# Placing all activation slots of a two-layer encoder in one stretch of SBUF

## The chip, the cores and the metric

The kernel runs on one core of one Trainium2 chip. The metric is the device time of one execution in microseconds. Beside the timed runs there is one profiled execution, whose trace is read below.

## What is computed

A conformer-style encoder with two layers on 256 positions of width D = 2048, all in float32:

```python
for i in range(2):
    h = rmsnorm(x, mix_norm[i])
    if i == 0:   # GLU convolution module: D -> 2D, 31 taps per channel, layernorm, silu, D -> D
        u = h @ w_in + b_in;  u = a * sigmoid(gate);  u = causal_dwconv31(u)
        m = silu(layernorm(u)) @ w_out + b_out
    else:        # differential attention, 16 heads, T5 bias, chunked mask
        m = diff_attention(h, w_qkv, ...) @ w_o
    x = x + m
    h = rmsnorm(x, ffn_norm[i])
    u = causal_dwconv3(h @ w_up)            # D -> 2 * 5632
    x = x + (silu(gate) * val) @ w_down     # 5632 -> D
return rmsnorm(x, final_norm_g)
```

## The kernel before

Activations lie channels by positions: a tile of 128 channels x 256 positions. Every large product is made in split precision. A float32 weight tile `raw` (128 x 1024, 512 KB) comes by DMA on SP's queue; ScalarE rounds it to `hi` (L160) and VectorE, or GpSimd in the convolution, stores the rest as `lo` (L164). An activation is split the same way into one tile of 128 x 2 x 256, the rounded part and the rest side by side (`split_act`, L290 and L291). Such a tile fills one activation slot of 2048 bytes a partition.

`pair` makes 256 output channels in one group of matmuls. For each of the 128 input channels and each half j it issues a main matmul (`hi` against all 512 columns of the activation tile, L249) and a correction (`lo` against the first 256, L250); for the last input tile the order is turned round (L246, then L247). A weight tile serves four input tiles and is one step. A group over the 16 input tiles has 4 steps and 32 main/correction couples; in the FFN's down projection a group has 8 input tiles and 16 couples (4 and 8 in the first chunk). The convolution's input projection uses three matmuls of 256 columns instead (L240).

In order the stages are: input projection and convolution, layernorm, output projection (8 groups), first FFN, attention, its output projection (8 groups), second FFN. An FFN has 44 groups up and six chunks of 8 groups down, interleaved: one chunk's 8 groups up, then the previous chunk's 8 groups down. All steps stand in one list; the framework's scheduler turns it into one order per engine and sets the waits.

Slots come from two pools. `acta` has 25 slots and is opened early. When it has none left (during the first output projection), `act_tile` closes the convolution's pool `ph1` and opens `ph2` (tables and tiles of attention) and `actb`, 8 more slots, in the place that the convolution had. From then on a tile takes a slot of `acta` if one is free, otherwise one of `actb`; the trace names them act and actb. At most 33 slots are in use.

Of the kernel before, what the change touches and what calls it, by code (L numbers as in the profile page):

```python
# [8 lines left out]
F32 = mybir.dt.float32  # L9
# [5 lines left out]
P = 128  # L15
S = 256
# [3 lines left out]
FK = 3  # L20
# [5 lines left out]
class Cfg:  # L26


    def __init__(self, d, f, kc=4):
        self.D, self.F = d, f  # L30
        self.KT = d // P
        self.FT = f // P
        self.H = d // (2 * HD)
        self.KC = kc
        self.NW = kc * 256
        self.kcs = [(i, kc) for i in range(0, self.KT, kc)]
        full = self.KT // 2
        first = self.FT % full or full
        self.chunks = [(0, first)] + [(i, full) for i in range(first, self.FT, full)]
        self.VK = kc // 2  # L40
        self.NA, self.NB = self.KT + self.KT // 2 + 1, 8

        self.G = [3] * (self.KT - 3) + [5, 6, 0]

        self.ND = 16
# [16 lines left out]
class Builder:  # L62
    def __init__(self, ctx, tc, cfg, a):
        self.tc, self.nc, self.c, self.a = tc, tc.nc, cfg, a
        ec = ctx.enter_context
        self.ctx = ctx
        self.const = ec(tc.tile_pool(name="const", bufs=1))
        self.rawp = ec(tc.tile_pool(name="rawp", bufs=5))
        self.hip = ec(tc.tile_pool(name="hip", bufs=6))
        self.lop = ec(tc.tile_pool(name="lop", bufs=6))  # L70
        self.acta = ec(tc.tile_pool(name="acta", bufs=cfg.NA))
        self.sm = ec(tc.tile_pool(name="sm", bufs=2))
        self.pp = ec(tc.tile_pool(name="pp", bufs=2, space=bass.MemoryType.PSUM))
        self.px = ec(tc.tile_pool(name="px", bufs=1, space=bass.MemoryType.PSUM))
        self.dr = ec(tc.tile_pool(name="dr", bufs=1, space=bass.MemoryType.DRAM))
        self.ph1_stack = ExitStack()
        self.ph1 = self.ph1_stack.enter_context(tc.tile_pool(name="ph1", bufs=2))
        self.actb = None
        self.na, self.nb = cfg.NA, 0
        self.coloff, self.ncol = cfg.cols()  # L80
        self.steps, self.W, self.todo = [], [], {}
        self.s = self.n = self.np_ = self.ns = 0
        self.every = self.pool_first = None
# [4 lines left out]


    def b2(self, tag, dt=F32):  # L90
        return self.sm.tile([P, 2, S], dt, tag=tag, name=self.nm(tag), bufs={"E": 4, "Y": 4, "Z": 2, "A": 2}[tag])

    def b1(self, tag):
        return self.sm.tile([P, S], F32, tag=tag, name=self.nm(tag), bufs={"G": 4, "O": 3, "M": 3}[tag])
# [17 lines left out]


    def act_tile(self, dt=F32R):
        if self.na > 0:
            self.na -= 1
            return ("a", self.acta.tile([P, 2, S], dt, tag="act", name=self.nm("act")))
        if self.actb is None:
            self.ph1_stack.close()
            self.ph2 = self.ctx.enter_context(self.tc.tile_pool(name="ph2", bufs=1))  # L120
            self.actb = self.ctx.enter_context(self.tc.tile_pool(name="actb", bufs=self.c.NB))
            self.nb = self.c.NB
        assert self.nb > 0
        self.nb -= 1
        return ("b", self.actb.tile([P, 2, S], dt, tag="actb", name=self.nm("actb")))

    def free(self, tiles):
        for w, _ in tiles:
            if w == "a":
                self.na += 1  # L130
            else:
                self.nb += 1


    def load_w(self):
# [275 lines left out]
    def setup(self, n0):  # L411
        nc, c, a = self.nc, self.c, self.a
        KT = c.KT
        self.X = [self.const.tile([P, 2, S], F32, name=f"x{pr}") for pr in range(KT // 2)]
        o1, o2 = self.coloff["cw"][0], self.coloff["cb"][0]
        self.prm = self.const.tile([P, self.ncol - o2 + o1], F32, name="prm")
        self.cprm = self.ph1.tile([P, o2 - o1], F32, name="cprm", bufs=1)
        nc.scalar.dma_start(self.prm[:, :o1], a["prm"][:, :o1])
        self.ones = self.const.tile([P, P], F32, name="ones")
        nc.vector.memset(self.ones, 1.0)  # L420
        nc.scalar.activation(self.c2(), self.ones[:, 0:2], AF.Sigmoid)
        self.mhalf = self.const.tile([P, 2], F32, name="mhalf")
        nc.vector.memset(self.mhalf, -0.5)

        warm = self.psx("t", [P, P])
        for _ in range(7):
            nc.tensor.matmul(warm, self.ones, self.ones, start=True, stop=True)
        for pr in range(KT // 2):
            if self.np_ < 5:
                list(self.load_w())  # L430
            (nc.scalar if pr < 2 else nc.sync).dma_start(self.X[pr], a["x"][:, 2 * pr:2 * pr + 2, :])
        self.ident = self.const.tile([P, P], F32, name="ident")
        nc.sync.dma_start(self.ident, a["ident"])
        nc.sync.dma_start(self.cprm, a["prm"][:, o1:o2])
        self.cmask = self.const.tile([P, 32], F32, name="cmask")
        nc.sync.dma_start(self.cmask, a["cmask"])
        nc.sync.dma_start(self.prm[:, o1:], a["prm"][:, o2:])
        with self.tc.manual_schedule(engines={ET.DVE, ET.Activation, ET.Pool}):
            for m in range(KT):
                if m in (0, 2):  # L440

                    first = self.split_w() if m == 0 else first
                    next(first)
                elif m % 4 == 0 and m < 12:
                    self.ahead(self.ns)
                n0["xh"][m] = self.act_tile()
                self.split_act(n0["xh"][m][1], self.X[m // 2][:, m % 2, :], self.col("mixg", m))
                if m % 4 == 3 and m < 12:
                    self.ahead(self.ns)
                if m % 4 == 3 and m > 4:  # L450
                    for pr in (m // 2 - 3, m // 2 - 2):
                        self.x_square(n0, pr)
            for pr in (KT // 2 - 2, KT // 2 - 1):
                self.x_square(n0, pr)

        self.todo[7] = [lambda: self.norm_cols(n0)]
        self.todo[8] = [lambda: self.norm_rows(n0)]
        self.fpad = []
        for i in range(2):
            t = self.const.tile([P, 2, S + FK - 1], F32, name=f"fpad{i}")  # L460
            nc.vector.memset(t[:, :, 0:FK - 1], 0.0)
            self.fpad.append(t)
        self.cpad = []
        for i in range(4):
            t = self.ph1.tile([P, S + CK + 1], F32, name=f"cpad{i}", bufs=1)
            nc.vector.memset(t[:, 0:CK - 1], 0.0)
            nc.vector.memset(t[:, S + CK - 1:], 0.0)
            self.cpad.append(t)


    def conv_module(self, nin, nout):
        c, a = self.c, self.a
        nc = self.nc
# [196 lines left out]
        def layernorm():  # L670
# [24 lines left out]
            nc.vector.tensor_tensor(mr, mean, rc, ALU.mult)  # L695

            rp = [self.psx("s", [P, S]) for _ in range(2)]
            rs = self.b2("E")
            for x, v in enumerate((rc, mr)):
                self.rows(rp[x], v)  # L700
# [129 lines left out]
    def attn_setup(self):  # L830

        nc, c, a = self.nc, self.c, self.a
        H = c.H
        rb = self.ph2.tile([NB, H], F32, name="rb")
        self.tc.keep_in_program_order(nc.gpsimd.dma_start(rb, a["relb"]))
        oh = self.b2("Z").rearrange("p a s -> p (a s)")[:NB, :384]
        nc.gpsimd.dma_start(oh, a["oneh"])
        ps = self.psx("o", [P, 384])
        nc.tensor.matmul(ps[:H, :], rb, oh, start=True, stop=True)
        tb = self.b2("Z").rearrange("p a s -> p (a s)")[:H, :384]  # L840
        nc.vector.tensor_copy(tb, ps[:H, :])
        tab = self.dr.tile([H, 384], F32, name="tab")
        nc.gpsimd.dma_start(tab, tb)
# [320 lines left out]
```

## Time and profile before

| what | value |
|---|---|
| median of 3 runs | 2229.67 us (2228.4 to 2231.36) |
| profiled execution, its own time | 2228.45 us |
| its span from first to last instruction | 2226.7 us |
| mean granted clock of TensorE | 0.997 |
| TensorE (PE) matmuls busy | 2202.7 us, 99% of the span |
| weight loads (PEld) busy | 1935.3 us, 87% |
| VectorE (DVE) busy | 1629.1 us, 73% |
| ScalarE (ACT) busy | 1200.9 us, 54% |
| GpSimd (POOL) busy | 251.1 us, 11% |
| HBM traffic | 187 GB/s over the span |

Matmuls overlap, and their ends in the trace are modelled; how fast the stream runs is read from the starts. Outside the span lie 1.75 us of the profiled execution's time.

### The profile page before, as it was taken

To read this page: it belongs to the slowest core of one execution; us is meant where nothing else is said; L and a number is where in the kernel's file an instruction comes from. 1 tells how busy PE (TensorE), PEld (TensorE's weight loads), DVE (VectorE), ACT (ScalarE), POOL (GpSimd) and SP (SyncE) were. 2 spreads that over 40 slices of the span, in tenths; PEclk is the share of its full clock that TensorE was granted. 3 is DMA by queue.
4 is the path that set the end of the run, shared out by engine and by line. 5 is a ranking of instruction groups with operands and counts; after the bars stand their busy time and mean duration, and the time that the engine had idled before them with its cause. 6 is when DMAs were issued, how large, how long until landed. Compare 5 with 4: busy or idle time off the path is not lost.

```text
span 2226.7 us, 34566 instructions
## 1 busy us (share of the span) xinstructions
PE 2202.7 (99%) x13274; PEld 1935.3 (87%) x13274; DVE 1629.1 (73%) x2482; ACT 1200.9 (54%) x1799; POOL 251.1 (11%) x175
## 2 busy tenths in 40 slices
PE   9999899999999999999999999999999999999998
PEld 8899788888888888888888888888888888888887
DVE  5888777787767677677687778767777677776774
ACT  5333555555555455555565555555555455554554
POOL 2987510000000000000100000100000000000002
PEclk9999999999999999999999999999999999999999
DMA  7876365666666656665655555556666566666652
GB/s 262 229 221 199 115 189 184 196 200 196 198 197 200 189 189 186 191 187 186 194 171 182 171 171 172 173 188 189 188 185 189 188 189 189 190 189 189 189 188 97
DMA packets 127317, 417.15 MB, mean 187 GB/s; under 512 B 14608, under 2 KB 28576, under 8 KB 127152
## 3 DMA queue, kind: packets, MB, share of 16 engines
q1 hardware_dynamic: 115584, 403.32, 58.2%
q10 hardware_dynamic: 11472, 11.54, 2.1%
q8 instruction: 104, 1.70, 0.3%
q14 instruction: 61, 0.50, 0.1%
q0 software_dynamic: 96, 0.08, 0.0%
HBM read 410.13 MB, written 7.33 MB: 187 GB/s over the span
## 4 chain that ended last, share of the span: by engine, by line
PE 95%; issue 2%; DVE 1%; POOL 1%; DMA 1%; ACT 0%; POOLq 0%; ACTq 0%
PE pp L249 49%; PE pp L250 25%; PE pp L240 6%; PE pp L247 4%; PE pp L246 2%; PE pp L900 1%; PE pp L902 1%; PE pp L901 1%; PE s L952 1%; PE s L542 1%; DMA R<-ud 1%; PE o L987 0%; POOL lo L164 0%; PE s L249 0%; DVE s L599 0%
## 5 line engine op out<-in xcount | busy, mean ns | idle before, releaser
L249 PE MATMUL pp<-act,hi 128*128 128x512 f32 x3902 | 1378.7, 395 | 1.6 <-ACT hi L160 1.1
L250 PE MATMUL pp<-act,lo 128*128 128x256 f32 x3902 | 1095.0, 281 | 0.0
L164 DVE TENSOR_TENSOR lo<-raw,hi 128x1024 fp32r<-128x1024 f32 (+1 forms) x693 | 849.8, 1228 | 286.7 <-ACT hi L160 285.2
L160 ACT CAST hi<-raw 128x1024 fp32r<-128x1024 f32 (+1 forms) x753 | 788.0, 1047 | 499.8 <-PE pp L249 190.9
L249 PEld LDWEIGHTS pp<-act,hi 128*128 128x128 f32 x3902 | 731.6, 187 | 161.5 <-ACT hi L160 1.4
L250 PEld LDWEIGHTS pp<-act,lo 128*128 128x128 f32 x3902 | 737.1, 189 | 9.8
L249 PE MATMUL pp<-actb,hi 128*128 128x512 f32 x856 | 306.9, 396 | 0.0
L250 PE MATMUL pp<-actb,lo 128*128 128x256 f32 x856 | 240.3, 281 | 0.0
L347 POOL TENSOR_TENSOR ssq<-ssq,Z 128x512 f32<-128x512 f32 x24 | 35.9, 1496 | 1549.1 <-ACT Z L343 1549.0
L249 PEld LDWEIGHTS pp<-actb,hi 128*128 128x128 f32 x856 | 160.6, 188 | 38.4 <-issue 0.6
L240 PE MATMUL pp<-act,hi 128*128 128x256 f32 x1024 | 188.5, 286 | 3.1 <-ACT act L290 1.9
L240 PEld LDWEIGHTS pp<-act,hi 128*128 128x128 f32 x1024 | 160.7, 193 | 9.4 <-issue 4.9
L277 ACT COPY E<-pp 128x512 f32<-128x512 f32 x104 | 60.9, 586 | 190.1 <-PE pp L247 190.1
L250 PEld LDWEIGHTS pp<-actb,lo 128*128 128x128 f32 x856 | 161.5, 189 | 0.2
L402 ACT COPY E<-pp 128x512 f32<-128x512 f32 x109 | 63.9, 586 | 170.3 <-PE pp L247 162.6
L279 DVE TENSOR_TENSOR E<-pp,E 128x512 f32<-128x512 f32 x104 | 71.9, 691 | 111.5 <-ACT E L277 111.5
L788 DVE SCALAR_TENSOR_TENSOR Y<-fpad,prm,Y 128x256 f32<-128x256 f32 x352 | 146.7, 477 | 0.0
L240 PE MATMUL pp<-act,lo 128*128 128x256 f32 x512 | 145.4, 284 | 0.3 <-DVE lo L164 0.3
L164 POOL TENSOR_TENSOR lo<-raw,hi 128x1024 fp32r<-128x1024 f32 x60 | 142.8, 2406 | 14.3 <-ACT hi L160 7.3
L404 DVE TENSOR_TENSOR x<-pp,x 128x512 f32<-128x512 f32 x101 | 69.7, 690 | 87.8 <-ACT E L402 87.4
L785 ACT ACTIVATE Y<-fpad,prm 128x256 f32<-128x256 f32 x176 | 96.3, 595 | 45.5 <-DVE fpad L781 45.5
L599 DVE SCALAR_TENSOR_TENSOR s<-cpad,cprm,s 128x256 f32<-128x256 f32 x182 | 85.2, 486 | 20.2 <-PE s L542 16.8
(214 smaller groups left out, 1846.9 us busy)
## 6 DMA issues: line engine op xcount, KB each, us to landing
raw<-in_w_up_dram SPq DMA_DIRECT2D x352, 512.0 KB, 3.7
raw<-in_w_down_dram SPq DMA_DIRECT2D x176, 512.0 KB, 3.7
raw<-in_w_qk_dram SPq DMA_DIRECT2D x64, 512.0 KB, 3.6
raw<-in_w_in_dram SPq DMA_DIRECT2D x63, 512.0 KB, 4.8
raw<-in_w_out_dram SPq DMA_DIRECT2D x32, 512.0 KB, 3.8
raw<-in_w_v_dram SPq DMA_DIRECT2D x32, 512.0 KB, 3.7
raw<-in_w_o_dram SPq DMA_DIRECT2D x32, 512.0 KB, 3.7
R<-ud ACTq DMA_DIRECT2D x52, 132.0 KB, 5.9
```

The costliest lines, as they stand in the source:

```text
L160: nc.scalar.copy(hi[:, p], raw[:, p])
L164: ins = eng.tensor_tensor(lo[:, p], raw[:, p], hi[:, p].bitcast(F32), ALU.subtract)
L240: nc.tensor.matmul(ps[:, 0:S], w[:, kk, cs], xt[:, x, :], start=(k == first and n == 0), stop=(k == last and n == 2))
L247: nc.tensor.matmul(*main, start=False, stop=True)
L249: nc.tensor.matmul(*main, start=(k == first), stop=False)
L250: nc.tensor.matmul(*corr, start=False, stop=False)
L279: nc.vector.tensor_tensor(t, ps[:, :, 0:S], cs, ALU.add)
L402: nc.scalar.copy(cs, ps[:, :, S:])
L404: nc.vector.tensor_tensor(x, ps[:, :, 0:S], x, ALU.add)
L599: nc.vector.scalar_tensor_tensor(acc, u[:, j:j + S], self.col("cw", i * CK + j), acc, ALU.mult, ALU.add)
L785: nc.scalar.activation(y[:, j, :], u[:, j, FK - 1:], AF.Identity, scale=self.col("fw", ch * FK + FK - 1), bias=self.col("fb", ch))
L788: nc.vector.scalar_tensor_tensor(y[:, j, :], u[:, j, q:q + S], self.col("fw", ch * FK + q), y[:, j, :], ALU.mult, ALU.add)
```

## The change

The 33 slots become one pool, opened directly behind `hi` and `lo`; `raw` moves behind it. `actb` is gone, and with it the switch in `act_tile`. The convolution's place is handed over explicitly (`second`, called in the layernorm once the statistics are known) to `ph2`, which now also holds the buffers of tags E and A (before in the pool `sm`) and `fpad` (before in `const`). The two clearings of `fpad` move from VectorE at the start to GpSimd in `attn_setup`.

```diff
-        self.NA, self.NB = self.KT + self.KT // 2 + 1, 8
+        self.NA = self.KT + self.KT // 2 + 9
...
-        self.rawp = ec(tc.tile_pool(name="rawp", bufs=5))
         self.hip = ec(tc.tile_pool(name="hip", bufs=6))
         self.lop = ec(tc.tile_pool(name="lop", bufs=6))
         self.acta = ec(tc.tile_pool(name="acta", bufs=cfg.NA))
+        self.rawp = ec(tc.tile_pool(name="rawp", bufs=5))
...
     def b2(self, tag, dt=F32):
-        return self.sm.tile([P, 2, S], dt, tag=tag, name=self.nm(tag), bufs={"E": 4, "Y": 4, "Z": 2, "A": 2}[tag])
+        pool = self.ph2 if tag in "EA" else self.sm
+        return pool.tile([P, 2, S], dt, tag=tag, name=self.nm(tag), bufs={"E": 4, "Y": 4, "Z": 2, "A": 2}[tag])
...
     def act_tile(self, dt=F32R):
-        if self.na > 0:
-            self.na -= 1
-            return ("a", self.acta.tile([P, 2, S], dt, tag="act", name=self.nm("act")))
-        if self.actb is None:
-            self.ph1_stack.close()
-            self.ph2 = self.ctx.enter_context(self.tc.tile_pool(name="ph2", bufs=1))
-            self.actb = self.ctx.enter_context(self.tc.tile_pool(name="actb", bufs=self.c.NB))
-            self.nb = self.c.NB
-        assert self.nb > 0
-        self.nb -= 1
-        return ("b", self.actb.tile([P, 2, S], dt, tag="actb", name=self.nm("actb")))
+        assert self.na > 0
+        self.na -= 1
+        return ("a", self.acta.tile([P, 2, S], dt, tag="act", name=self.nm("act")))
...
+    def second(self):
+
+        self.ph1_stack.close()
+        self.ph2 = self.ctx.enter_context(self.tc.tile_pool(name="ph2", bufs=1))
...
-        self.fpad = []
-        for i in range(2):
-            t = self.const.tile([P, 2, S + FK - 1], F32, name=f"fpad{i}")
-            nc.vector.memset(t[:, :, 0:FK - 1], 0.0)
-            self.fpad.append(t)
...
             rp = [self.psx("s", [P, S]) for _ in range(2)]
+            self.second()
             rs = self.b2("E")
...
     def attn_setup(self):
...
+        self.fpad = []
+        for i in range(2):
+            t = self.ph2.tile([P, 2, S + FK - 1], F32, name=f"fpad{i}")
+            nc.gpsimd.memset(t[:, :, 0:FK - 1], 0.0)
+            self.fpad.append(t)
```

Where the buffers lie, in bytes of a partition, as the two built programs place them:

| buffers | before | after |
|---|---|---|
| `raw` (5 x 4096) | 46,048 to 66,528 | 158,624 to 179,104 |
| `hi` (6 x 4096) | 66,528 to 91,104 | 41,888 to 66,464 |
| `lo` (6 x 4096) | 91,104 to 115,680 | 66,464 to 91,040 |
| act | 25 slots, 115,680 to 166,880 | 33 slots, 91,040 to 158,624 |
| `sm` | 166,880 to 202,112 | 179,104 to 202,048 |
| `ph1`, then `ph2` | 202,112 and up | 202,048 and up |
| actb | 8 slots, 211,392 to 227,776 | none |

On TensorE the order of the matmuls is the same in both programs; only the slots that they read differ. The rows are from a group of the first FFN's up projection, where before it passes from the slots of one pool to those of the other (pp is the group's PSUM tile, hi and lo a step's split weights). Before:

```order
L249 MATMUL pp_4578<-act_3661,hi_4511 128x512
L250 MATMUL pp_4578<-act_3661,lo_4512 128x256
L249 MATMUL pp_4578<-actb_3671,hi_4511 128x512
L250 MATMUL pp_4578<-actb_3671,lo_4512 128x256
L249 MATMUL pp_4578<-actb_3671,hi_4511 128x512
L250 MATMUL pp_4578<-actb_3671,lo_4512 128x256
```

The same place now (line numbers are 5 lower):

```order
L244 MATMUL pp_4575<-act_3661,hi_4508 128x512
L245 MATMUL pp_4575<-act_3661,lo_4509 128x256
L244 MATMUL pp_4575<-act_3664,hi_4508 128x512
L245 MATMUL pp_4575<-act_3664,lo_4509 128x256
L244 MATMUL pp_4575<-act_3664,hi_4508 128x512
L245 MATMUL pp_4575<-act_3664,lo_4509 128x256
```

The next input tile, which was in actb, is now in the one pool; nothing moved in the order.

On GpSimd three instructions move. The rows are those just ahead of the layernorm's power (M holds sums of the statistics, c the variance, L694 before and L684 now is the power). Before:

```order
L164 TENSOR_TENSOR lo_2932<-raw_2706,hi_2931 128x1024
L659 TENSOR_TENSOR M_2926<-M_2926,O_2961 128x256
L694 TENSOR_TENSOR c_3031<-c_3030,mhalf 128x2
L164 TENSOR_TENSOR lo_3159<-raw_2760,hi_3158 128x1024
L164 TENSOR_TENSOR lo_3182<-raw_2830,hi_3181 128x1024
```

Now:

```order
L159 TENSOR_TENSOR lo_2928<-raw_2702,hi_2927 128x1024
L649 TENSOR_TENSOR M_2922<-M_2922,O_2957 128x256
L828 MEMSET fpad_3978 128x2x2
L828 MEMSET fpad_3980 128x2x2
L831 DMA rb<-in_relb_dram 32x16
L684 TENSOR_TENSOR c_3027<-c_3026,mhalf 128x2
L159 TENSOR_TENSOR lo_3159<-raw_2756,hi_3158 128x1024
```

The scheduler has put the two clearings of `fpad` and the load of the bias table `rb` (before some 100 us later) ahead of the power. The first clearing waits until VectorE's and TensorE's last reads of the convolution's tiles are done. Beside this, one ScalarE eviction (L911) and its VectorE twin (L913) in the attention stand behind one or two more weight splits than before; SP's order is the same.

## Rows read from the trace of the kernel before

**Rows 1.** The page: busy time of each engine, and shares of the last-ending chain.

```profile
PE 2202.7 (99%) x13274; PEld 1935.3 (87%) x13274; DVE 1629.1 (73%) x2482; ACT 1200.9 (54%) x1799; POOL 251.1 (11%) x175
...
PE 95%; issue 2%; DVE 1%; POOL 1%; DMA 1%; ACT 0%; POOLq 0%; ACTq 0%
```

**Rows 2.** Busy time by stretch: first FFN, second FFN; length, engines, PEclk, DMA.

```profile
337.00:1100.00 763.00, 763.00 (x4358) 667.17 (x4357) 559.99 (x750) 420.30 (x572) 12.42 (x11) 1.00 0.62 192
...
1416.00:2210.00 794.00, 794.00 (x4548) 694.87 (x4547) 577.92 (x764) 438.36 (x602) 17.98 (x12) 1.00 0.59 184
```

**Rows 3.** TensorE's waits, the longest in total: us, times, longest.

```profile
PE s L542 <- DMA R<-ud: 2.7, 2, 1.8
```

**Rows 4.** Timeline, TensorE: first matmuls of groups, output projection, no actb.

```profile
281.99 0.40 PE L249 MATMUL pp<-act,hi 128*128 128x512 f32 x1
...
293.10 0.39 PE L249 MATMUL pp<-act,hi 128*128 128x512 f32 x1
...
304.40 0.39 PE L249 MATMUL pp<-act,hi 128*128 128x512 f32 x1
...
338.30 0.39 PE L249 MATMUL pp<-act,hi 128*128 128x512 f32 x1
```

**Rows 5.** Groups of TensorE instructions in 281.99:293.09, then in 293.10:304.39.

```profile
L249 PE MATMUL pp<-act,hi 128*128 128x512 f32 x30 | 10.5, 391 | 0.0
...
L249 PE MATMUL pp<-act,hi 128*128 128x512 f32 x30 | 10.6, 398 | 0.0
```

**Rows 6.** First FFN, up: group starts seven groups apart, and 407.82:418.98 by line.

```profile
385.49 0.40 PE L249 MATMUL pp<-act,hi 128*128 128x512 f32 x1
...
463.66 0.40 PE L249 MATMUL pp<-act,hi 128*128 128x512 f32 x1
...
L249 PE MATMUL pp<-act,hi 128*128 128x512 f32 x18 | 6.3, 391 | 0.0
...
L249 PE MATMUL pp<-actb,hi 128*128 128x512 f32 x12 | 4.3, 396 | 0.0
```

**Rows 7.** Timeline, TensorE: starts of three groups, second FFN, up.

```profile
1642.31 0.40 PE L249 MATMUL pp<-act,hi 128*128 128x512 f32 x1
...
1653.43 0.39 PE L249 MATMUL pp<-act,hi 128*128 128x512 f32 x1
...
1664.71 0.40 PE L249 MATMUL pp<-act,hi 128*128 128x512 f32 x1
```

**Rows 8.** Timeline, TensorE: starts of three groups down, no actb.

```profile
1726.27 0.39 PE L249 MATMUL pp<-act,hi 128*128 128x512 f32 x1
...
1731.83 0.39 PE L249 MATMUL pp<-act,hi 128*128 128x512 f32 x1
...
1737.47 0.39 PE L249 MATMUL pp<-act,hi 128*128 128x512 f32 x1
```

**Rows 9.** Timeline, TensorE: starts of two groups down, with actb in each.

```profile
1866.24 0.40 PE L249 MATMUL pp<-act,hi 128*128 128x512 f32 x1
...
1871.82 0.40 PE L249 MATMUL pp<-act,hi 128*128 128x512 f32 x1
```

**Rows 10.** The chain of waits, convolution's input projection: start, us, matmuls of a group.

```profile
147.23 11.71 PE pp L240 x96
160.37 11.71 PE pp L240 x96
```

**Rows 11.** Timeline of the layernorm: GpSimd and VectorE ahead of the power.

```profile
231.76 0.72 POOL L659 TENSOR_TENSOR M<-M,O 128x256 f32<-128x256 f32 x1
...
234.67 1.36 DVE L873 MEMSET kd<- 64x256 f32 x4 [0.27 <-DMA raw<-in_w_out_dram]
...
238.60 0.70 POOL L694 TENSOR_TENSOR c<-c,mhalf 128x2 f32<-128x2 f32 x1 [6.12 <-DVE c L693]
```

**Rows 12.** GpSimd: its load of the table in the timeline, its clearings by line.

```profile
336.27 0.72 POOL L835 DMA_DIRECT2D rb<-in_relb_dram  x1 [2.07 <-issue]
...
L941 POOL MEMSET bm<- 64x64 f32 x16 | 2.3, 144 | 160.4 <-DMA bm<-d 98.6 <-DVE lo L164 29.8 <-DVE A L969 16.6
```

More of the change, by code (lines that the diff above doesn't have):

```diff
@@ L77, in __init__ @@
         self.ph1 = self.ph1_stack.enter_context(tc.tile_pool(name="ph1", bufs=2))
-        self.actb = None
-        self.na, self.nb = cfg.NA, 0
+        self.ph2 = None
+        self.na = cfg.NA
         self.coloff, self.ncol = cfg.cols()
@@ L114, in act_tile @@
     def act_tile(self, dt=F32R):
-        if self.na > 0:
-            self.na -= 1
-            return ("a", self.acta.tile([P, 2, S], dt, tag="act", name=self.nm("act")))
-        if self.actb is None:
-            self.ph1_stack.close()
-            self.ph2 = self.ctx.enter_context(self.tc.tile_pool(name="ph2", bufs=1))
-            self.actb = self.ctx.enter_context(self.tc.tile_pool(name="actb", bufs=self.c.NB))
-            self.nb = self.c.NB
-        assert self.nb > 0
-        self.nb -= 1
-        return ("b", self.actb.tile([P, 2, S], dt, tag="actb", name=self.nm("actb")))
-    def free(self, tiles):
[L128 to L132, printed above, removed]
+        assert self.na > 0
+        self.na -= 1
+        return ("a", self.acta.tile([P, 2, S], dt, tag="act", name=self.nm("act")))
+    def free(self, tiles):
+        self.na += len(tiles)
+    def second(self):
+        self.ph1_stack.close()
+        self.ph2 = self.ctx.enter_context(self.tc.tile_pool(name="ph2", bufs=1))
     def load_w(self):
```

## The prediction

> **What bounds the kernel now.** First the page: TensorE is busy 99% of the span and carries 95% of the chain that ended last [rows 1]. Then the stretches: in both FFNs PE is busy for the whole stretch, 763.00 of 763.00 us and 794.00 of 794.00, at full granted clock [rows 2]. Then PE's waits: the longest in total is 2.7 us [rows 3]. So no slot that comes free earlier can save much. What counts is how fast the stream of main and correction matmuls runs, and that shows only in the starts.
>
> Starts of equal groups are not equally far apart. In the output projection, where every input lies in `acta`, one group of 32 couples takes 293.10 − 281.99 = 11.11 us and the next, with the same instructions, 304.40 − 293.10 = 11.30; the three after it 33.90 / 3 = 11.30 each [rows 4]. PE idles in none of them; the main matmul's mean is 391 ns in the first and 398 in the second [rows 5]. The stream has two beats, **fast** (11.11 a group, 347 ns a couple) and **slow** (11.30, 353 ns). A beat lasts a whole group, and what follows is regular: a fast group is followed by a slow one, and a slow group of 32 couples by another slow one [rows 4]. In a down group of 16 couples the slow beat stops at another point of its cycle, and the beats alternate: 5.56, then 5.64 [rows 8].
>
> Where inputs lie in actb it goes otherwise. In the first FFN a group up reads 18 couples from act and then 14 from actb (12 of them on L249): the mean is 391 in the first part, 396 in the second. Every such group starts fast again, so that seven take (463.66 − 385.49) / 7 = 11.167 us each [rows 6]. In the second FFN actb comes last in a group; a slow group that ends there is followed by a fast one, and the two alternate: 11.12 and 11.28, mean 11.20 [rows 7]. Down groups with actb in them take 5.58 each [rows 9], 5.60 being the mean without it [rows 8]. Reading from actb thus costs some nanoseconds at once, and it resets the beat for the next group.
>
> **The change part by part.**
>
> *Matmuls off the actb slots.* The order on PE is unchanged; all inputs now lie between 91,040 and 158,624, and the reset is gone. I take it that every slot of the new stretch reads as the acta slots do. The new addresses of `hi` and `lo`, up to 24,640 bytes lower, and of some slots are in no row; the nearest rows are the convolution's groups, where four of the six `hi` and `lo` slots serve each group in turn, and every group takes the same 11.71 us [rows 10]. So within the old range the slot does not matter. From below, the cost of the new addresses is nothing; from above, that they keep the slow beat everywhere.
>
> Then an up group is followed as in rows 4: slow after slow. First FFN: 44 groups, less three that the norm's and the set-up's matmuls break into: 41 × (11.30 − 11.167) = +5.5 us. Second FFN: 44 less two: 42 × (11.30 − 11.20) = +4.2. Of the 96 down groups, 16 have actb in them; they go from 5.58 to alternating 5.56 and 5.64: 16 × 0.02 = +0.3. The other down groups alternate as before, only the first one's beat changes, and eight groups bring four of each. Attention's output projection has a few groups with actb, on both beats already: I take 0 for it. Conv, output projection and attention's head groups hold next to no actb: 0. Sum +10.0 us.
>
> *The handover in the layernorm.* PE stands still there, so GpSimd's queue matters. Its last sum ends at 231.76 + 0.72 = 232.48, and the power starts at 238.60 after idling 6.12 us for VectorE [rows 11]. Into this gap go two clearings and the load of `rb`. The first clearing waits for the same last reads of the convolution as VectorE's clearing of `kd`, which started at 234.67 [rows 11]. A GpSimd clearing takes 144 ns in L941, the load 0.72 us, with or without the 2.07 us of issue ahead of it [rows 12]. So they end between 234.67 + 0.29 + 0.72 = 235.7 and 237.8; taking 0.72 us a clearing (the M sum of rows 11 has far more elements) and the 2.07, 238.9. Only this last is late, by 0.3 us, and behind the power wait the row statistics and the whole stage. I take 0, with 0.3 for the range. Were the gap not there, the load and the clearings would cost their 1.0 to 4.2 us on the path.
>
> *Clearings off VectorE, E and A in `ph2`, the closing of `ph1` earlier.* The clearings ran at the start, while weights were still on their way; each is a few columns. The tiles of E that take the place of convolution tiles wait for reads that ended before the layernorm's statistics; the copy into E waits for the power anyway. The L911 eviction in attention comes at most two weight casts later, and its PSUM buffer is wanted only a group of 11 us later [rows 7]. All 0: PE does not idle there [rows 1].
>
> *Sum.* 2228.45 + 10.0 = 2238.5 for an execution like the profiled one, which lies 1.2 us under the median of 2229.67; the median would go to 2239.7. I say **2239 us**, +0.4%. About 0.2% (4.5 us) is what a measurement of this kernel can tell from no change.
>
> **The rivals.**
>
> *No change, 2229.* The beat would come from something other than the address, and the slow and fast groups keep their shares. For it: down groups change beat without any actb [rows 8]. Against: up groups of both FFNs have the same instructions and differ in their lengths as the place of actb in the group does [rows 6, 7], and the couples slow down within the group where actb begins [rows 6]. The Trainium skill, page "SBUF — State Buffer", section "Who interferes with whom", says that PE and ACT never wait on anyone at their SBUF ports, and names no address that reads slower; by that page this rival would hold. Rows 6 speak against it as far as addresses go.
>
> *Faster, 2219.* Moving the weights too lets every group begin on the fast beat. It decides at the end of a slow group of 32 couples: if the next starts fast, the slow beat dies out. Up: 41 × (11.167 − 11.11) = 2.3 and 42 × (11.20 − 11.11) = 3.8; down: 64 groups at 5.56 in place of 5.60 = 2.6, and 16 × 0.02 = 0.3; output projection 5 × 0.19 = 1.0. Sum −10.0. For it: the weights' addresses do move, and no row shows PE reading from there. Against: four slow groups in a row with nothing from actb [rows 4].
>
> *Slower still, 2243.* The low weight slots cost what actb costs, or the first group of each chunk stays slow: then down groups all take 5.64, 64 × 0.04 + 16 × 0.06 − 0.3 = +3.3 us on top of the 10.0. Against: the steady 11.71 of rows 10.
>
> *A late power* adds at most 0.3 us to any case (above).
>
> **How the numbers follow.** Forecast 0.60: the beat's rule rests on clean rows, but its transfer to new addresses is untested. No change 0.17, faster 0.15, slower still 0.08. The likeliest one's own range is 2236 to 2242 (second FFN's share and the broken groups by 2 us either way, 1.2 us between profile and median). The range of 8 in 10 takes in no change and slower still: 2228 to 2243; it leaves out the faster case. Faster by over 0.2%: 0.15; within: 0.17; slower: 0.68.
>
> **What would show it.** Groups up in both FFNs 11.30 us apart from the second or third of a chunk on, with main matmuls at a mean of 398 ns and no part at 391; down groups alternating 5.56 and 5.64 everywhere; convolution groups still 11.71; PE's busy time up by 10 us with its idle time the same. On GpSimd the power still starts just behind VectorE's last step, with `rb` ahead of it. The prediction is wrong if up groups still come at 11.17 or 11.20, if they come at 11.11, or if the convolution's 11.71 moves, which would mean that the weights' addresses count.

## The result, and the profile after

| what | before | after |
|---|---|---|
| median | 2229.03 us (2226.8 to 2231.36, 4 runs) | 2241.8 us (2240.77 to 2242.89, 4 runs) |
| profiled execution, its own time | 2228.45 us | 2242.1 us |
| its span | 2226.7 us | 2240.3 us |

The four runs of the kernel before are the three ahead of the prediction and one more. The ratio is 1.0054, with a 95% interval of 1.0042 to 1.0066: the change makes the kernel 0.5% slower. The page after, busy time by engine, answers to [rows 1]:

```profile
PE 2213.8 (99%) x13274; PEld 1938.5 (87%) x13274; DVE 1632.6 (73%) x2480; ACT 1201.3 (54%) x1799; POOL 251.4 (11%) x177
```

PE has as many matmuls as before and is 11.1 us longer busy with them; the rest of the span grew too, from 24.0 to 26.5 us. The timeline of TensorE after, first matmuls of groups: two in the output projection [rows 4], two in the first FFN seven groups apart [rows 6], two in the second FFN [rows 7], and three down groups, of which the first held actb before [rows 9]. Lines are 5 lower than before.

```profile
285.31 0.39 PE L244 MATMUL pp<-act,hi 128*128 128x512 f32 x1
...
296.61 0.39 PE L244 MATMUL pp<-act,hi 128*128 128x512 f32 x1
...
389.06 0.39 PE L244 MATMUL pp<-act,hi 128*128 128x512 f32 x1
...
468.16 0.39 PE L244 MATMUL pp<-act,hi 128*128 128x512 f32 x1
...
1528.20 0.39 PE L244 MATMUL pp<-act,hi 128*128 128x512 f32 x1
...
1539.50 0.39 PE L244 MATMUL pp<-act,hi 128*128 128x512 f32 x1
...
1877.92 0.39 PE L244 MATMUL pp<-act,hi 128*128 128x512 f32 x1
...
1883.57 0.39 PE L244 MATMUL pp<-act,hi 128*128 128x512 f32 x1
...
1889.12 0.39 PE L244 MATMUL pp<-act,hi 128*128 128x512 f32 x1
```

Seven groups up take 468.16 − 389.06 = 79.10 us, 11.30 each, where they took 11.167; the second FFN's group takes 11.30, and its down groups alternate 5.65 and 5.55. The groups of instructions in 389.06:400.35 show what [rows 5] showed of a slow group:

```profile
L244 PE MATMUL pp<-act,hi 128*128 128x512 f32 x30 | 10.6, 398 | 0.0
```

The chain of waits shows the convolution's 11.71 of [rows 10] unmoved:

```profile
147.46 11.71 PE pp L235 x96
```

These are the two beats of the prediction, the slow one now in nearly all up groups. A second loss stands in the layernorm. The timeline of GpSimd, then of VectorE, from the clearings to the first norm (L699), after:

```profile
235.05 0.14 POOL L828 MEMSET fpad<- 128x4 f32 x2 [2.04 <-PE o L292]
235.63 0.72 POOL L831 DMA_DIRECT2D rb<-in_relb_dram  x1 [0.44 <-issue]
239.33 0.72 POOL L684 TENSOR_TENSOR c<-c,mhalf 128x2 f32<-128x2 f32 x1 [2.98 <-DVE c L683]
240.03 4.63 POOL L159 TENSOR_TENSOR lo<-raw,hi 128x1024 fp32r<-128x1024 f32 x2
...
240.08 2.30 DVE L685 TENSOR_TENSOR c<-mom,c 128x2 f32<-128x2 f32 x1 [0.85 <-POOL c L684]
242.31 2.38 DVE L851 TENSOR_TENSOR c<-prm 64x2 f32<-64x2 f32 x1
244.61 1.71 DVE L699 TENSOR_TENSOR act<-act,s 128x256 f32<-128x256 f32 x4
```

The same instructions of VectorE before (L695 is L685 now, L855 is L851, L708 is L699):

```profile
239.34 2.29 DVE L695 TENSOR_TENSOR c<-mom,c 128x2 f32<-128x2 f32 x1 [0.82 <-POOL c L694]
241.55 0.14 DVE L855 TENSOR_TENSOR c<-prm 64x2 f32<-64x2 f32 x1
241.62 0.40 DVE L708 TENSOR_TENSOR act<-act,s 128x256 f32<-128x256 f32 x1
```

The product of 64 x 2 values (`lm`, L851) takes 0.14 us before and 2.38 after, and the first norm stands behind it on VectorE. From the power to the first norm it is 244.61 − 239.33 = 5.28 us; before, with the power of [rows 11], 241.62 − 238.60 = 3.02. So the first norm comes 2.26 us later. Each small product that takes 2.3 us lies beside one of GpSimd's two weight subtractions, which read SBUF and take 4.63 / 2 = 2.3 us each, and each has both its inputs in SBUF. The Trainium skill, page "SBUF — State Buffer", section "Who interferes with whom", has that rule: a VectorE instruction with two inputs in SBUF and a GpSimd instruction that reads SBUF exclude each other, and the later one blocks for the whole of the other. The trace agrees in the two lengths: 0.14 us free, 2.38 held. Which of the two gets ahead the starts do not tell: before and after, that of the 64 x 2 product stands 0.02 us ahead of the second subtraction's (241.55 and 241.57, then 242.31 and 242.33). The first norm, whose second input `s` is in PSUM, takes its 0.40 us beside the same subtraction before.

The account of the profiled executions: 0.7 us ahead of the power, 2.3 from the power to the first norm, 0.3 from there to the group just ahead of [rows 4], and 10.2 from that group's start (270.81 before, 274.13 after) to the last group's (1931.14 us later before, 1941.39 after). Together 13.6, the difference of the spans.

### The profile page after: what moved, and what is told of

Read it like the earlier page. It is cut to its first block, busy times and chain, and to the rows that moved or that the text cites. A ratio compares the mean times of both kernels' runs of the same rounds, so it can differ in the third digit from the quotient of the medians.

```text
span 2240.3 us, 34571 instructions
## 1 busy us (share of the span) xinstructions
PE 2213.8 (99%) x13274; PEld 1938.5 (87%) x13274; DVE 1632.6 (73%) x2480; ACT 1201.3 (54%) x1799; POOL 251.4 (11%) x177
## 4 chain that ended last, share of the span: by engine, by line
PE 94%; issue 2%; DMA 1%; DVE 1%; POOL 1%; ACT 0%; POOLq 0%; ACTq 0%
PE pp L244 49%; PE pp L245 25%; PE pp L235 6%; PE pp L242 4%; PE pp L241 2%; PE pp L896 1%; PE pp L897 1%; PE pp L898 1%; PE s L948 1%; PE s L532 1%; POOL lo L159 0%; PE o L983 0%; DMA R<-ud 0%; DMA raw<-in_w_in_dram 0%; PE s L556 0%
## 5 line engine op out<-in xcount | busy, mean ns | idle before, releaser
L244 PE MATMUL pp<-act,hi 128*128 128x512 f32 x4758 | 1689.1, 398 | 4.9 <-DVE act L715 3.8
L245 PE MATMUL pp<-act,lo 128*128 128x256 f32 x4758 | 1337.3, 281 | 0.0
L244 PEld LDWEIGHTS pp<-act,hi 128*128 128x128 f32 x4758 | 894.1, 188 | 211.6 <-DVE act L715 4.3
L245 PEld LDWEIGHTS pp<-act,lo 128*128 128x128 f32 x4758 | 899.5, 189 | 10.1
L235 PEld LDWEIGHTS pp<-act,hi 128*128 128x128 f32 x1024 | 161.9, 194 | 9.0 <-issue 4.9
L242 PE MATMUL pp<-act,hi 128*128 128x512 f32 x426 | 158.8, 396 | 0.0
L235 PE MATMUL pp<-act,lo 128*128 128x256 f32 x512 | 145.9, 285 | 0.0
L241 PE MATMUL pp<-act,lo 128*128 128x256 f32 x426 | 120.0, 282 | 0.0
L235 PEld LDWEIGHTS pp<-act,lo 128*128 128x128 f32 x512 | 99.3, 194 | 0.4 <-issue 0.4
L242 PEld LDWEIGHTS pp<-act,hi 128*128 128x128 f32 x426 | 80.3, 189 | 10.1
```

The costliest lines, as they stand in the source:

```text
L235: nc.tensor.matmul(ps[:, 0:S], w[:, kk, cs], xt[:, x, :], start=(k == first and n == 0), stop=(k == last and n == 2))
L241: nc.tensor.matmul(*corr, start=False, stop=False)
L242: nc.tensor.matmul(*main, start=False, stop=True)
L244: nc.tensor.matmul(*main, start=(k == first), stop=False)
L245: nc.tensor.matmul(*corr, start=False, stop=False)
```

## The experiments

The first four ask whether the place of the slots or of the weights, the second pool or the order of the couples makes the beat, and whether the `lm` product is the layernorm's loss. Each kernel is the changed one with the edit shown, unless said otherwise.

**Weights back.** `raw` is opened first again, so `hi` starts at 62,368 and the slots at 111,520.

```diff
+        self.rawp = ec(tc.tile_pool(name="rawp", bufs=5))
         self.hip = ec(tc.tile_pool(name="hip", bufs=6))
         self.lop = ec(tc.tile_pool(name="lop", bufs=6))
         self.acta = ec(tc.tile_pool(name="acta", bufs=cfg.NA))
-        self.rawp = ec(tc.tile_pool(name="rawp", bufs=5))
```

> The changed kernel with the raw weights' pool opened ahead of the split weights again: hi and lo return to within 4 KB of where they stood before, every activation slot stays in one stretch (111,520 to 179,104 bytes). Address theory (only the place of the moving activations decides the beat, and the high stretch alone disturbs it): nothing changes, every 32-couple group of the first FFN 11.30 us, time 2242 us within 1.5. Rival, the split weights' new places make the slow beat: the groups go back to 11.11 to 11.17 us and the time to about 2232 us.

Measured 2242.49 us (2242.12 to 2243.41). The timeline of TensorE, group starts seven groups apart as above:

```profile
388.58 0.39 PE L244 MATMUL pp<-act,hi 128*128 128x512 f32 x1
...
467.68 0.39 PE L244 MATMUL pp<-act,hi 128*128 128x512 f32 x1
```

79.10 / 7 = 11.30. Nothing changed. It looks like a point for the place of the slots; seen from the end, it is not, because weights and slots moved together.

**`lm` later.** One VectorE instruction is put behind the layernorm.

```diff
-        nc.vector.tensor_tensor(lm[:HD], self.col("lam", 0, 2)[:HD], self.col("lam", 2, 2)[:HD], ALU.mult)
+        self.tc.keep_in_program_order(nc.vector.tensor_tensor(lm[:HD], self.col("lam", 0, 2)[:HD], self.col("lam", 2, 2)[:HD], ALU.mult))
```

> The changed kernel with one VectorE instruction moved: the 64x2 product lm<-prm is issued in program order behind the 16x384 copy of the bias table, so after the layernorm, no longer between the mean times rstd product and the first norm. Port theory (this instruction, with two inputs in SBUF, lost the port to GpSimd's second lo subtraction and waited 2.24 us, and the first norm waited behind it): the first norm starts about 2.2 us earlier and the time falls by 2.2 us against the changed kernel, to about 2239.7. Rival (the first norm, which reads SBUF too, loses to the same subtraction in its place, or the handover is bound by the rows on TensorE): no change, 2241.8.

Measured 2240.17 us (2238.52 to 2241.84, 5 runs), 1.6 under the changed kernel, with ranges that overlap; the time alone does not settle 2 us. The timeline of GpSimd and VectorE does:

```profile
238.77 0.72 POOL L684 TENSOR_TENSOR c<-c,mhalf 128x2 f32<-128x2 f32 x1 [3.01 <-DVE c L683]
...
241.75 0.41 DVE L699 TENSOR_TENSOR act<-act,s 128x256 f32<-128x256 f32 x1
```

241.75 − 238.77 = 2.98 us from the power to the norm, as before the change, and the norm itself is not held.

**No turned couple.** The last input tile's couples come in the order of the others (`stop` moves to the correction).

```diff
-                if k == last:
-                    nc.tensor.matmul(*corr, start=False, stop=False)
-                    nc.tensor.matmul(*main, start=False, stop=True)
-                else:
-                    nc.tensor.matmul(*main, start=(k == first), stop=False)
-                    nc.tensor.matmul(*corr, start=False, stop=False)
+                nc.tensor.matmul(*main, start=(k == first), stop=False)
+                nc.tensor.matmul(*corr, start=False, stop=(k == last))
```

> The changed kernel with the last tile's couples in the order of all others: main, then correction (before: correction, then main, so that two mains meet where groups meet). Beat theory (a beat lasts until something breaks the alternation; the turned couple at the group's end breaks it and picks the next group's beat): without it the beat of the first group stays for the whole stage. If that is the fast one: up groups 11.11 us, down groups 5.556 throughout, about 83 x 0.19 + 38 x 0.088 = 19 us less, 2223. If the slow one: all 11.30 and 5.65, 2242 to 2245. Rival, the beat is set by something else than the order of the couples (addresses of weights or slots of the group): the groups keep their 11.30 and the 5.64/5.56 alternation, 2242.

Measured 2246.07 us, with a wide spread (2238.93 to 2252.97). Group starts, eight groups apart ahead of the first FFN's first down groups, then four apart behind them:

```profile
379.93 0.39 PE L240 MATMUL pp<-act,hi 128*128 128x512 f32 x1
...
468.68 0.39 PE L240 MATMUL pp<-act,hi 128*128 128x512 f32 x1
...
538.31 0.40 PE L240 MATMUL pp<-act,hi 128*128 128x512 f32 x1
...
583.54 0.40 PE L240 MATMUL pp<-act,hi 128*128 128x512 f32 x1
```

88.75 / 8 = 11.09, then 45.23 / 4 = 11.31. With the same addresses both beats can run, and without the turned couple each goes on for many groups. Neither forecast of one beat for a whole stage came true: in both FFNs the beat turns slow around the first, small down groups, where TensorE waits up to 0.8 us at a time. The four times stand in two pairs, near 2240 and near 2252; that they differ in where the beat turns is not shown, as one execution alone was profiled. In the changed kernel, by this run, it is the turned couple that makes a fast group hand on the slow beat, as in [rows 4], and so the up groups end up slow all alike.

**Slots high.** The slots' pool is opened last but one: still one pool, now at 134,464 to 202,048.

```diff
-        self.acta = ec(tc.tile_pool(name="acta", bufs=cfg.NA))
         self.rawp = ec(tc.tile_pool(name="rawp", bufs=5))
         self.sm = ec(tc.tile_pool(name="sm", bufs=2))
+        self.acta = ec(tc.tile_pool(name="acta", bufs=cfg.NA))
```

> The changed kernel with the slots' pool opened last but for the stage's own pool: still one pool of 33 slots, but at 134,464 to 202,048 bytes rather than 91,040 to 158,624. Address theory: where slots above the boundary (somewhere from 166,880 to 211,392, by the kernel before) are read, the beat alternates 346 and 361 ns from the second couple after, and groups that hold such slots give the next group the fast beat: if the boundary lies low in that span, a part or all of the up groups take 11.11 to 11.25 us and the time is 2232 to 2240; if it lies above 202,048, all stay 11.30 and the time 2242. Rival, the second pool itself (its semaphores or the order in which slots are handed out) and not its place made the fast groups: all 11.30 us, 2242, whatever the boundary.

Measured 2216.0 us (2214.26 to 2216.43), ratio to before 0.9935 (0.992 to 0.995): faster than both. The same two group starts:

```profile
384.47 0.39 PE L244 MATMUL pp<-act,hi 128*128 128x512 f32 x1
...
462.17 0.39 PE L244 MATMUL pp<-act,hi 128*128 128x512 f32 x1
```

77.70 / 7 = 11.10. Neither theory allowed that. Every group that runs undisturbed is fast. The slots now share 134,464 to 166,880 with the place of `acta` before, where groups ran slow, so a boundary between low and high does not explain it. What sets this pool apart is its start: 134,464 is 64 x 2101, as 211,392, the start of actb, is 64 x 3303; 91,040, 111,520 and 115,680, the starts of all other slots so far, are 32 more than a multiple of 64. That gave the theory for the next four.

**A gap of 32 bytes.** An unused tile between weights and slots; all else is as changed.

```diff
         self.lop = ec(tc.tile_pool(name="lop", bufs=6))
+        ec(tc.tile_pool(name="gap", bufs=1)).tile([P, 8], F32, name="gap")
         self.acta = ec(tc.tile_pool(name="acta", bufs=cfg.NA))
```

> The changed kernel with an unused 32-byte tile between the split weights and the slots: each slot starts at 91,072 + 2048 n, a multiple of 64 bytes, rather than at 91,040 + 2048 n, 32 past one; nothing else of the program moves. Multiple-of-64 theory (the slots of the second pool before, at 211,392, and those of the run with slots high, at 134,464, start on multiples of 64 bytes; the slots of every slow beat start 32 past one): every whole group of 32 couples takes 11.10 us and of 16 couples 5.55, and the time is that of the run with slots high, 2216, 26 us under the changed kernel. Rival, the stretch of SBUF (slots high up, away from the split weights, are read faster): slots still lie low, all groups stay 11.30, time 2242.

Measured 2216.8 us (2214.97 to 2219.51), ratio 0.9941 (0.9924 to 0.9957). Group starts, then the convolution's groups in the chain of waits:

```profile
382.23 0.39 PE L245 MATMUL pp<-act,hi 128*128 128x512 f32 x1
...
460.03 0.39 PE L245 MATMUL pp<-act,hi 128*128 128x512 f32 x1
```

```profile
92.69 11.40 PE pp L236 x96
```

77.80 / 7 = 11.11. 32 bytes are worth 25 us against the changed kernel: 20.7 in the groups from the one ahead of those in [rows 4] to the last (1920.72 for 1941.39), and most of the rest in the convolution, whose groups fall from 11.71 to 11.40.

**Slots high with the gap.** The same tile ahead of the slots of the kernel with slots high, which then start at 134,496.

> The run with the slots high, with the 32-byte tile ahead of its slots: they start at 134,496 + 2048 n, 32 past a multiple of 64, and stay in the same high stretch. Multiple-of-64 theory: the slow beat is back, groups 11.30 us, time 2242 (26 above the run with slots high). Rival, the stretch of SBUF: all groups stay 11.10, time 2216.

Measured 2239.5 us (2237.48 to 2242.16). Group starts, then the convolution's groups in the chain of waits:

```profile
381.29 0.40 PE L245 MATMUL pp<-act,hi 128*128 128x512 f32 x1
...
460.35 0.40 PE L245 MATMUL pp<-act,hi 128*128 128x512 f32 x1
```

```profile
93.52 11.10 PE pp L236 x96
```

79.06 / 7 = 11.29: slow again, in the same high stretch. But the convolution's groups became faster still, 11.10, which nothing had foretold; here the gap moved the slots to 64 bytes, modulo 128, from the weights (the remainder that a division of the distance by 128 leaves).

**The kernel before, its second pool moved by 32 bytes.** The tile goes ahead of actb alone, which then starts at 211,424.

```diff
             self.ph2 = self.ctx.enter_context(self.tc.tile_pool(name="ph2", bufs=1))
+            self.ctx.enter_context(self.tc.tile_pool(name="gap", bufs=1)).tile([P, 8], F32, name="gap")
             self.actb = self.ctx.enter_context(self.tc.tile_pool(name="actb", bufs=self.c.NB))
```

> The kernel before with the 32-byte tile ahead of its second pool alone: the eight slots at 211,392 move to 211,424, 32 past a multiple of 64, as its other slots are; they stay in the high stretch and in a pool of their own. Multiple-of-64 theory: nothing sets the beat back any more, up groups of the first FFN 11.30 us, of the second 11.30 instead of 11.12 and 11.28 in turn, time 2229.7 + 10.2 = 2240. Rival, the high stretch itself: groups stay 11.17, time 2229.7 within 1.5.

Measured 2238.96 us (2238.78 to 2239.31), ratio 1.0038 (1.0023 to 1.0053). Group starts:

```profile
385.69 0.39 PE L250 MATMUL pp<-act,hi 128*128 128x512 f32 x1
...
464.79 0.39 PE L250 MATMUL pp<-act,hi 128*128 128x512 f32 x1
```

79.10 / 7 = 11.30. This is the loss of the change, from the groups alone, in the layout of before: 8.6 us over the kernel before's 2230.34 on the same chip, and 10.7 from the group ahead of those in [rows 4] to the last (1941.80 for 1931.14).

**The gap ahead of the weights.** The tile stands before `hip`, so that weights (41,920) and slots (91,072) both start on a multiple of 64.

> The changed kernel with the 32-byte tile ahead of the split weights, so that hi, lo and the slots all start on multiples of 64 bytes (in the run with the tile behind the weights only the slots do). Multiple-of-64 theory for the moving operand alone: as that run, groups 11.10 us, 2216. Rival, the weights' loads gain too: groups below 11.10 us, for example the full 11.00, and the time below 2210.

Measured 2241.39 us (2239.78 to 2244.12). Group starts:

```profile
387.14 0.39 PE L245 MATMUL pp<-act,hi 128*128 128x512 f32 x1
...
466.24 0.39 PE L245 MATMUL pp<-act,hi 128*128 128x512 f32 x1
```

11.30: slow, with slots on multiples of 64. Both expectations fell, and no run shows groups of 11.00. The slots' own start does not decide; what is left is their start relative to the weights, or the weights' own.

**The mirror image.** One tile ahead of the weights and one ahead of the slots: weights on a multiple of 64 (41,920), slots 32 past one (91,104).

> The changed kernel with a 32-byte tile ahead of the split weights and another ahead of the slots: hi and lo start on multiples of 64 bytes, the slots 32 past one, the mirror image of the run with one tile behind the weights. Difference theory (the slow beat comes where weights and moving slots have the same rest modulo 64 bytes, as 32 and 32 in the changed kernel or 0 and 0 in the run with the tile ahead of the weights; with different rests all groups are fast): groups 11.10 us, about 2216. Rival, the slots themselves must start on a multiple of 64 and the weights must not: groups 11.30, 2241.

Measured 2216.44 us (2214.57 to 2217.03). Group starts:

```profile
380.65 0.39 PE L246 MATMUL pp<-act,hi 128*128 128x512 f32 x1
...
458.44 0.39 PE L246 MATMUL pp<-act,hi 128*128 128x512 f32 x1
```

77.79 / 7 = 11.11: fast, with the weights on a multiple of 64 as in the slow run before it. The difference decides.

**The kernel before with all slots moved.** One tile ahead of `acta`, one ahead of `actb`; the slots start at 115,712 and 211,456, in two stretches as before.

> The kernel before with a 32-byte tile ahead of each of its two pools of slots, so that all its slots start on multiples of 64 and its weights 32 past one; the two stretches of slots stay. Difference theory: whether slots stand in one stretch or two is worth nothing; all groups 11.10 us, and without the 2.3 us that the lam product waits in the layernorm the time is 2213 to 2217, 13 to 17 under the kernel before. Rival, one stretch is worth something by itself once the beats are equal: over 2218, with groups of 11.17 where the high slots are read.

Measured 2216.01 us (2211.91 to 2217.51), ratio 0.9938 (0.9924 to 0.9952). Group starts, and `lm` on VectorE:

```profile
378.69 0.39 PE L251 MATMUL pp<-act,hi 128*128 128x512 f32 x1
...
456.48 0.39 PE L251 MATMUL pp<-act,hi 128*128 128x512 f32 x1
...
236.56 0.14 DVE L857 TENSOR_TENSOR c<-prm 64x2 f32<-64x2 f32 x1
```

11.11, as with the slots in one stretch; from the group ahead of those in [rows 4] to the last it is 1920.65 us, with the gap in the one stretch 1920.72. One stretch or two is worth nothing. Here `raw`, `hi` and `lo` stand where they stood before and only the slots and what lies behind them moved, so the fast beat needs no new place of the weights either.

**The small products off VectorE.** The kernel with the 32-byte gap, `lm` later as above, and the product mean times rstd on GpSimd behind the power.

```diff
-            self.pool_first = nc.gpsimd.tensor_tensor(rc, v, self.mhalf, ALU.pow).ins
-            nc.vector.tensor_tensor(mr, mean, rc, ALU.mult)
+            nc.gpsimd.tensor_tensor(rc, v, self.mhalf, ALU.pow)
+            self.pool_first = nc.gpsimd.tensor_tensor(mr, mean, rc, ALU.mult).ins
```

> The changed kernel with the 32-byte tile between weights and slots, the lam product behind the layernorm, and the 128x2 product mean times rstd on GpSimd straight behind the power, ahead of the two lo subtractions, so that neither small product stands on VectorE while GpSimd subtracts. Port theory: the first norm starts 0.8 to 1.5 us after the power instead of 5.3, of which the rows on TensorE hide nothing: 2.3 us (lam) and 1.5 to 2.2 us (mean times rstd) less than the run with the tile alone, about 2212.5. Rival, the norms on VectorE, which read SBUF too, then wait for the first subtraction in their turn: 2214.5, only the lam part gained.

Measured 2214.49 us (2213.51 to 2215.46, 5 runs), ratio 0.9934 (0.9921 to 0.9948): the lowest median of all, but not apart from the 2216.8 with the gap alone, as their ranges overlap. The timeline of GpSimd and VectorE:

```profile
235.48 0.72 POOL L685 TENSOR_TENSOR c<-c,mhalf 128x2 f32<-128x2 f32 x1 [3.63 <-DVE c L684]
236.28 0.19 POOL L686 TENSOR_TENSOR c<-mom,c 128x2 f32<-128x2 f32 x1
236.44 4.65 POOL L160 TENSOR_TENSOR lo<-raw,hi 128x1024 fp32r<-128x1024 f32 x2
...
238.03 0.42 DVE L700 TENSOR_TENSOR act<-act,s 128x256 f32<-128x256 f32 x1 [2.64 <-PE s L299]
```

The product takes 0.19 us and is done 1.0 us after the power's start, 2.1 sooner than in the changed kernel (240.08 + 2.30 − 239.33 = 3.05). The norm still starts 2.55 us after it, for now it waits for the row statistics on TensorE (L299). They had been hidden behind the held product; against the 2.98 with `lm` later, 0.4 us is left as gain, not the 1.5 to 2.2 expected. The time is the rival's 2214.5, but not for its reason: the norm takes 0.42 us and is not held by the subtraction beside it.

**`lo` apart.** A tile between `hi` and `lo` and one between `lo` and the slots: hi 41,888, lo 66,496, slots 91,104.

> The changed kernel with a 32-byte tile between hi and lo and another between lo and the slots: hi and slots start 32 past a multiple of 64 as in the changed kernel, lo alone on a multiple. The lo weights are loaded while a main matmul (512 columns) reads its slot, the hi weights while a correction (256 columns) does. If the rest modulo 64 of the load beside the longer read decides: the groups are fast, 11.10 to 11.11 us, time 2216. If that of the load beside the correction decides: all groups 11.30, 2242. If each adds its own part: groups between, 11.2, and about 2229.

Measured 2224.62 us (2222.95 to 2226.6), ratio 0.998 (0.997 to 0.999). Group starts:

```profile
386.24 0.40 PE L246 MATMUL pp<-act,hi 128*128 128x512 f32 x1
...
464.40 0.40 PE L246 MATMUL pp<-act,hi 128*128 128x512 f32 x1
```

78.16 / 7 = 11.17, between the beats: modulo 128 the slots now lie 64 from `hi` and 32 from `lo`, where both at 64 gave 11.29 and both at 32 gave 11.11. So both loads seem to count, as the third forecast has it; its 2229 is 4 us too high. It is no clean split: against the changed kernel both distances are new, and the run with both at 64 has its slots elsewhere.

All layouts, by the start of the slots less that of the weights, modulo 128 bytes. The column of the convolution has TensorE's time for a group's 96 matmuls; up and down are means over all groups of a kernel that ran without interruption, from start to start (95 of 32 couples, 76 of 16):

| kernel | slots less weights | conv group | up group | down group | median us |
|---|---|---|---|---|---|
| after; weights back; `lm` later | 0 | 11.71 | 11.30 | 5.60 | 2241.8; 2242.5; 2240.2 |
| gap ahead of the weights | 0 | 11.71 | 11.30 | 5.60 | 2241.4 |
| before, second pool moved | 0 | 11.71 | 11.30 | 5.60 | 2239.0 |
| before | 0, actb 96 | 11.71 | 11.19 | 5.60 | 2229.0 |
| gap; mirror image; before, all slots moved; small products off VectorE | 32 | 11.40 | 11.11 | 5.57 | 2216.8; 2216.4; 2216.0; 2214.5 |
| slots high | 32 | 11.46 | 11.10 | 5.55 | 2216.0 |
| slots high with the gap | 64 | 11.10 | 11.29 | 5.64 | 2239.5 |
| `lo` apart | 64, lo 32 | 11.49 | 11.17 | 5.58 | 2224.6 |

For instance before: 115,680 − 66,528 = 49,152 = 384 x 128; with the gap: 91,072 − 41,888 = 49,184, 32 more.

## Why the prediction was right, and where its reason was wrong

**The two beats and what follows a slow group: right.** First FFN: predicted +5.5 us, measured +5.4; second FFN with its down groups: +4.2 and a part of 0.3, measured +4.5; attention and output projection: 0, measured +0.1 and +0.2. The sum +10.0 came out as +10.2.

**"Reading from actb costs some nanoseconds at once, and it resets the beat": right as a pattern, wrong as a property of those slots.** The pattern vanishes when the same eight slots move by 32 bytes (before, second pool moved), and a single stretch of slots gets the fast beat when it moves by 32 bytes (gap). What set them apart was their distance from the weights, 96 bytes modulo 128, where the `acta` slots have 0. The rest modulo 64, which gave the runs their forecasts, is not all of it: 96 leaves the same rest as 32, but at 96 the main matmuls take 396 ns [rows 6], and at 32, in the same place of a group with all slots of before moved, 390. No run had all its slots at 96. The table of addresses ahead of the prediction held the number; the text read it as low and high.

**"I take that every slot of the new stretch reads as the acta slots do", and the weights' new addresses at nothing: right by luck.** Weights and slots both moved by 24,640 bytes, so their distance stayed 49,152. The convolution's rows, which varied the weights' slot, could not have shown the effect: those slots are 4096 bytes apart, the same modulo 128. With 32 bytes more between the two the sign turns, as the gap shows, and the rival "faster, 2219" comes true with all groups fast, though not for its reason, the weights' new place. "No change" falls with the 11.30, and "slower still" (its +3.3 adds up to 3.2) with the 11.71 and with down groups that still alternate.

**The handover in the layernorm, taken at 0 and at most 0.3: the step that failed, by 2.3 us.** The clearings and `rb` did end in the gap (235.63 + 0.72, the power at 239.33) and delayed nothing. What was not looked at is what their move does behind the power. There the `lm` product meets GpSimd's second subtraction: 0.14 us in the three kernels with the queue of before (before and its two variants), 2.37 to 2.39 in the nine traces with the changed queue and `lm` in its place. So it is no accident of one execution, and with `lm` moved the loss is gone. TensorE shows it too: from the power's start to that of the group ahead of those in [rows 4] it is 31.6 to 32.2 us in the three kernels with the queue of before and with `lm` later, and 33.5 to 34.8 where the product is held (eight traces; without the turned couple the groups are not the same). Why the subtraction now gets ahead of the product is only inferred: in the new order it waits for one event instead of two, as GpSimd has waited for TensorE already at the clearing. Keeping the clearings on VectorE was not tried.

**The median.** 2241.8 against 2239: 2.3 of the 2.8 are the layernorm's by the profiled executions, and the rest is within the scatter of executions.

**What stays open.** Why the distance counts at all: the runs show that it does, not how TensorE's reads of weights and of moving data meet in SBUF. Open, too, is why of the distances tried 32 is best for couples of 512 and 256 columns and 64 for the convolution's three of 256, and why slots high and the gap differ a little at the same 32 (11.10 and 11.11, 11.46 and 11.40); modulo 256 these two stand at 160 and 32, so 128 need not be the whole period. A layout that gives each stage its best distance was not tried; by the table, as an estimate, it could save the convolution's 11.40 − 11.10 = 0.3 us a group on top.

## What to carry to other kernels

Where TensorE never idles, compare the starts of equal groups: equal work with unequal lengths says that something other than waits sets the rate, here 1.7% of a stage. When the same operand is read at two rates, tabulate start addresses modulo small powers of two, of both operands, before thinking of near and far; a layout change can then be tried for the price of an unused 32-byte tile. And when work is moved onto GpSimd's queue, look at what follows it there too, and at which small VectorE instruction with two SBUF inputs stands beside its long ones.

## What the hardware showed that was not expected

TensorE's rate depends on the distance of its two operands in SBUF: a main and a correction matmul together take 347 or 353 ns (11.11 or 11.30 us for 32), with no wait recorded. At a distance of 0 modulo 128 both rates can go on for many groups, and the order of the couples moves the stream from one to the other; at 32 every full group of 32 couples was fast, at 64 slow. In all, 32 bytes moved the kernel by 25 us, where the change as given moved it by 13.
